# Rounded products for the query and key/value projections, and more weight halves split by an adding DMA

## The chip, the cores and the metric

The kernel runs on one core of one Trainium2 chip, as one launch. The metric is device time in microseconds (us), the median of several runs. All matrix products are done by TensorE (PE in the profile), elementwise work by VectorE (DVE) and ScalarE (ACT), transfers from the chip's memory (HBM) by 16 DMA engines; SyncE (SP) and GpSimd (POOL) only issue transfers here, apart from a few memsets.

## What is computed

Two networks stand one behind the other: a block with a convolution branch, an attention branch and a convolved feed-forward network, then a two-layer network with attention and a linear recurrence. Only the first part of the first block is touched by the change:

```python
h = rms_norm(x, norm1_g[l])
proj = h @ w_in[l]
a_in, q_c, kv_c, k_rope_in, gates = split_cols(proj, IN_SPLITS)
y_conv = conformer_conv(a_in, ...)          # gate, 31-tap depthwise conv, layer norm, silu, w_conv_out
# mla: 8 heads, q and kv from normalised low-rank parts
q  = (rms_norm(q_c, q_norm_g) @ w_uq)       # 384 -> 8 heads of 96
kv = (rms_norm(kv_c, kv_norm_g) @ w_ukv)    # 256 -> 8 heads of 64 + 64
...
g = jax.nn.sigmoid(gates)
merged = g[..., :D_MODEL] * y_conv + g[..., D_MODEL:] * y_mla
```

There are 256 tokens of width 1024; everything is float32.

## The kernel before

**Weights as one stream.** Every weight matrix is cut into blocks of 128 x 128, and the blocks lie in HBM (`wall`) in the order in which TensorE uses them (`PLAN`, L190). Sixteen blocks are a unit (1 MB) and eight a half (512 KB). `Stream` (L219) loads units into three buffers named `raw` (L229, issued by SP), and makes of each half two tiles `wh` and `wl` (L285, six buffers of each). `wh` is the weight rounded to the format fp32r, `wl` the rest that the rounding left out.

**Three rounded products or one native.** `product` (L442) takes a block and an operand that has been split in the same way into `xh` and `xl`, and issues three matmuls: wh by xh, wl by xh, wh by xl. For the matrices in `NATIVE` (L35: `w_uq` and `w_ukv`) the half is not split: the tile `raw` itself is multiplied by the unsplit operand in one float32 matmul, which TensorE runs as two records in the trace. The raw buffer of such a half becomes free only when TensorE has taken its last block (L349), that of a split half when the split is done (L314).

**Two ways to split.** Normally ACT rounds the half into `wh` (L254) and DVE subtracts (L255). For a half in `BY_DMA` (L307 to L311) ACT rounds it (L308) and writes the negative of the rounded half into `wl` (L309), and then POOL issues a DMA that reads the same half from HBM again and adds it on the way in, so that DVE has nothing to do.

**Looking ahead.** `ahead(look)` (L331) is called before and after the eight blocks of a column. It issues the splits of as many halves as `look` allows beyond the half in use: 4 as a rule (`LOOK`), 6 for `w_uq`, `w_ukv` and the gates (`N_SPLIT`). A split can start on the chip only when the half six places earlier has been used up, since there are six buffers.

**Order.** TensorE and SP run in the order of the program. For ACT, DVE and POOL a planner orders the instructions when the kernel is built; instructions marked by `paced` (L612) keep their order among each other. The 31 convolution taps of each of 4 channels (L621, on DVE) are taken from a list a few at a time, after each column of matmuls (`n_bg`, from `NB`), and they are paced.

**The stretch in question**, by halves in their order of use:

| halves | what TensorE does | lines |
|---|---|---|
| 0 to 7 | value and gate columns of the convolution branch (`w_a`) | L631 |
| 8 to 13 | five columns for `qc` and one for the rotary key | L668, L681 |
| 14 to 16 | `w_uq`, 8 heads of 3 blocks, native | L711 |
| 17, 18 | `w_ukv`, keys (256 wide) and values (512 wide), native | L721, L729 |
| 19 to 34 | 16 gate columns `w_g`, two after each head's scores | L817, L824 |
| 35 to 38 | `w_mla`, in a group of 4 columns and four of 1 | L859 |
| 39 on | `w_co`, the convolution branch's output | L861 |

After the `w_a` columns the query and key/value factors (`csq`, `kvr`, L691) are worked out by short ACT and DVE steps. The query factor is multiplied in afterwards (L714), while the key/value part of `qc` is multiplied beforehand (L699), so that `w_ukv` can only start behind it. Each head's and each gate's result has a PSUM buffer of its own (eight buffers of 512 columns, of which 256 are used), one DVE instruction that takes it out (L714, L821), and for the gates a tanh on ACT (L822).

**The layer norm of the convolution** is `ln_mean` (L791), ahead of `w_mla`, and `ln_rest` (L800), which TensorE meets between two groups of `w_mla` (`norm_conv`, L839: ahead of the first block of the group that begins with column 4). `ln_rest` sums the squares `usq` by TensorE, and then a chain on ACT and DVE ends in the split of `cacc` into `uh` and `ul`, which `w_co` needs.

Of the kernel before, what the change touches and what calls it, by code (L numbers as in the profile page):

```python
# [13 lines left out]
ALU = mybir.AluOpType  # L14
# [4 lines left out]
P = 128  # L19
D = 1024  # L20
S = 256
# [6 lines left out]
HB = 8  # L28
N_RAW = 3
N_SPLIT = 6  # L30
# [1 line left out]
GELU_AT = 4  # L32
Y_AT = {4: (0,), 5: (1, 2), 6: (3, 4, 5), 7: (6, 7)}
REC_GATES = {5: (0, 1, 2), 6: (3, 4), 7: (5, 6)}
NATIVE = {"w_uq", "w_ukv"}  # L35

DMA_GATES = (0, 3, 5, 7, 9, 11, 13, 14, 15)
NB = (3, 3, 2, 1, 5, 6)
WARM = 12
SCAN_N = 2  # L40
# [7 lines left out]
HEADS = 8  # L48
# [163 lines left out]


ITEMS = items()
GATE0 = next(i for i, e in enumerate(PLAN) if e[0] == "w_g") // HB
BY_DMA = {GATE0 + m for m in DMA_GATES}


class Stream:  # L219
# [135 lines left out]
def build(tc, wall, x_t, meta_t, pos, vec, cst, gw, g_fin, out):  # L355
    nc = tc.nc
    ctx = ExitStack()
    with ctx:
# [55 lines left out]
        def split(src, hi, lo):  # L414
            nc.scalar.copy(out=hi, in_=src)
            nc.vector.tensor_tensor(out=lo, in0=src, in1=hi.bitcast(F32), op=ALU.subtract)  # L416
# [15 lines left out]
        def tt(out_, a, b, op=ALU.mult):  # L432
            return nc.vector.tensor_tensor(out=out_, in0=a, in1=b, op=op)  # L433
# [18 lines left out]
        def linear(name, col, xs, nk, out_, n_bg=0, look=LOOK):  # L452
            w.ahead(look)
            for k in range(nk):
                product(out_, (name, k, col), xs(k), k == 0, k == nk - 1)
            w.ahead(look)
            for _ in range(min(n_bg, len(bg))):
                bg.popleft()()
# [153 lines left out]
        def paced(i):  # L612
            tc.stamp_issue_order_token(i.ins, "conv")
# [53 lines left out]

        for m in range(5):  # L668
            p_ = mm_tile()
            linear("w_a", m * P, xa, 8, p_[:, :S], n_bg=NB[1])  # L670
            g = v("q_norm_g", m) if m < 3 else v("kv_norm_g", m - 3)
            act(out=qc[:, m, :], in_=p_[:, :S], func=AF.Identity, scale=g)
            s_ = pt([P, S], "sqq", bufs=3)
            act(out=s_, in_=p_[:, :S], func=AF.Square)
            if m < 3 and "w_uq" not in NATIVE:
                split(qc[:, m, :], qh[:, m, :], ql[:, m, :])
            if m > 1:
                add_sq(m - 2)
            sqs.append(s_)
        kr_p = mm_tile()  # L680
        linear("w_a", 5 * P, xa, 8, kr_p[:, :S], n_bg=NB[1])  # L681
        csr = pt([P, S], "csr")
        tt(csr, cs, rstd[:, :S])
        krp = pt([P, S], "krp")
# [10 lines left out]
            rsqrt_row(q[:, :S], dst, n)  # L695
        tt(csq, csq, csr)
        tt(kvr, kvr, rstd[:, :S])
        for m in range(3, 5):
            tt(qc[:, m, :], qc[:, m, :], kvr)  # L699
            if "w_ukv" not in NATIVE:  # L700
                split(qc[:, m, :], qh[:, m, :], ql[:, m, :])

        def xq(k):
            return qc[:, k, :] if "w_uq" in NATIVE else (qh[:, k, :], ql[:, k, :])
# [3 lines left out]

        tables("exp_and_others")

        for h in range(HEADS):  # L711
            p_ = mm_tile()
            linear("w_uq", h * P, xq, 3, p_[:, :S], n_bg=NB[2], look=N_SPLIT)
            paced(stt(qp[:, h, :], p_[:, :S], MLA_SCALE, csq, ALU.mult, ALU.mult))  # L714

        kr2 = psum("tr", 2)
        mm(kr2[:, :S], c("comb"), krp, True, True)
# [96 lines left out]
                    split(cacc[:, k, :], uh[:, k, :], ul[:, k, :])  # L814

        es, pts = {}, {}
        def gate_out(i):  # L817
            p_ = mm_tile()
            linear("w_g", (14 + i) * P, xa, 8, p_[:, :S], n_bg=NB[4 + (i > 3)], look=N_SPLIT)
            dst = t1[:, i, :] if i < 8 else t2[:, i - 8, :]  # L820
            paced(tt(dst, p_[:, :S], rstd[:, :S]))  # L821
            act(out=dst, in_=dst, func=AF.Tanh, scale=0.5)  # L822

        for h in range(8):  # L824
            es[h] = scores(h)
            if h % 2 and h > 1:
                pv_mla((h - 3) // 2)
            if h:
                pts[h - 1] = transposes(es.pop(h - 1))
            gate_out(2 * h)  # L830
            gate_out(2 * h + 1)
        while bg:
            bg.popleft()()
        pts[7] = transposes(es.pop(7))
# [2 lines left out]
        uh, ul = pt([P, 5, S], "qh", F32R), pt([P, 5, S], "ql", F32R)  # L837

        def norm_conv(m, k):  # L839
            if m == 4 and k == 0:  # L840
                ln_rest()

        mh, ml = ph.tile([P, 8, S], F32R, tag="kp", name="mh"), ph.tile([P, 8, S], F32R, tag="qp", name="ml")
# [665 lines left out]
```

## Time and profile before

| | |
|---|---|
| device time, median of 3 runs | 964.12 us (963.01 to 965.53) |
| the profiled execution's own time | 966.51 us |
| its span | 964.7 us, 17922 instructions |
| mean granted TensorE clock | 0.997 |
| DMA | 168.58 MB, mean 175 GB/s |

The span is cut into 40 slices on the page; each digit is the busy share of the slice in tenths. The stretch in question lies in slices 2 to 7 (24 us each), and DVE is the busiest engine beside TensorE there:

```profile
PE   9998999999999999999999999999999999999997
PEld 8988999999999999999999999999999999998886
DVE  6997978799999665866786555455577986667986
ACT  7758868677666655555556666444469776776552
```

Busy time of TensorE in this profile includes the overlap of pipelined matmuls, so the waits and the chain that ended last say more than its share. Times in the views count from the start of the span.

### The profile page before, as it was taken

How to read it: one execution, taken by the hardware profiler on the slowest of the kernel's cores; microseconds unless marked ns; L12 is line 12 of the kernel's file. 1: busy time of each engine (PE TensorE's matmuls, PEld its weight loads, DVE VectorE, ACT ScalarE, POOL GpSimd, SP SyncE). 2: the span in 40 equal slices, each digit the busy share in tenths (PEclk: the TensorE clock that was granted, in tenths of full speed). 3: DMA queues.
4: the chain of work that ended last, by engine and by line, in shares of the span. 5: the costliest groups of instructions: out<-in, count | busy, mean ns of one | idle time of the engine just before them, and what ended most of it. 6: DMA issues, size and time to landing. Idle time of an engine off the chain costs nothing.

```text
span 964.7 us, 17922 instructions
## 1 busy us (share of the span) xinstructions
PE 949.8 (98%) x7315; PEld 916.7 (95%) x7315; DVE 728.1 (75%) x1264; ACT 614.8 (64%) x1042; POOL 14.5 (2%) x47
## 2 busy tenths in 40 slices
PE   9998999999999999999999999999999999999997
PEld 8988999999999999999999999999999999998886
DVE  6997978799999665866786555455577986667986
ACT  7758868677666655555556666444469776776552
POOL 0001100000000000000000000000000000000000
PEclk9999999999999999999999999999999999999999
DMA  8559844546545555332325554445443465563561
GB/s 307 201 147 295 211 151 157 186 167 214 179 176 188 191 191 175 132 127 96 128 97 209 175 175 176 176 175 175 175 175 132 141 237 191 175 207 127 197 212 44
DMA packets 27874, 168.58 MB, mean 175 GB/s; under 512 B 4048, under 2 KB 6032, under 8 KB 8720
## 3 DMA queue, kind: packets, MB, share of 16 engines
q1 hardware_dynamic: 25312, 160.29, 47.1%
q0 software_dynamic: 1584, 6.29, 3.1%
q10 hardware_dynamic: 896, 0.86, 0.4%
q8 instruction: 57, 0.93, 0.4%
q14 instruction: 25, 0.20, 0.1%
HBM read 165.92 MB, written 1.05 MB: 173 GB/s over the span
## 4 chain that ended last, share of the span: by engine, by line
PE 91%; DVE 4%; DMA 2%; ACT 2%; issue 0%; SPq 0%; DVEq 0%; ACTq 0%; POOLq 0%
PE ps_mm L439 85%; PE ps_z L439 3%; PE ps_o L439 1%; DMA wl<-wall 1%; DVE wl L255 1%; DMA raw<-wall 1%; PE ps_tr L439 1%; DVE iu L1231 0%; ACT L400 0%; DMA vec_t<-vec 0%; PE ps_tr L770 0%; DVE gt L433 0%; ACT wh L254 0%; DVE iu L433 0%; DVE th L436 0%
## 5 line engine op out<-in xcount | busy, mean ns | idle before, releaser
L255 DVE TENSOR_TENSOR wl<-raw,wh 128x1024 fp32r<-128x1024 f32 (+1 forms) x287 | 343.4, 1201 | 162.3 <-ACT wh L254 161.3
L254 ACT CAST wh<-raw 128x1024 fp32r<-128x1024 f32 (+1 forms) x287 | 293.6, 1030 | 192.8 <-PE ps_mm L439 185.1
L439 PE MATMUL ps_mm<-Ah,wh 128*128 128x256 f32 (+1 forms) x1424 | 408.9, 287 | 1.0 <-ACT Ah L404 1.0
L439 PE MATMUL ps_mm<-Ah,wl 128*128 128x256 f32 (+1 forms) x1424 | 405.1, 285 | 3.1 <-DMA wl<-wall 3.1
L439 PE MATMUL ps_mm<-Al,wh 128*128 128x256 f32 (+1 forms) x1424 | 403.8, 284 | 0.0
L439 PEld LDWEIGHTS ps_mm<-Ah,wl 128*128 128x128 f32 x1424 | 268.4, 188 | 4.0 <-DMA wl<-wall 3.3
L439 PEld LDWEIGHTS ps_mm<-Ah,wh 128*128 128x128 f32 x1424 | 267.9, 188 | 2.0 <-ACT Ah L404 1.4
L439 PEld LDWEIGHTS ps_mm<-Al,wh 128*128 128x128 f32 x1424 | 269.3, 189 | 0.4 <-DVE Al L424 0.4
L439 PE MATMUL ps_mm<-hl,wh 128*128 128x272 f32 (+1 forms) x432 | 123.5, 286 | 0.0
L439 PE MATMUL ps_mm<-hh,wh 128*128 128x272 f32 (+1 forms) x432 | 123.5, 286 | 0.0
L439 PE MATMUL ps_mm<-hh,wl 128*128 128x272 f32 (+1 forms) x432 | 123.3, 285 | 0.0
L439 PEld LDWEIGHTS ps_mm<-hh,wl 128*128 128x128 f32 x432 | 81.3, 188 | 0.0
L439 PEld LDWEIGHTS ps_mm<-hh,wh 128*128 128x128 f32 x432 | 81.3, 188 | 0.0
L439 PEld LDWEIGHTS ps_mm<-hl,wh 128*128 128x128 f32 x432 | 81.3, 188 | 0.0
L621 DVE SCALAR_TENSOR_TENSOR cacc<-upad,whalf,cacc 128x256 f32<-128x256 f32 x120 | 57.4, 479 | 2.0
L404 ACT ACTIVATE ta<-ps_mm 128x272 f32<-128x272 f32 (+1 forms) x64 | 25.0, 391 | 49.9 <-PE ps_mm L439 49.8
L439 PE MATMUL ps_mm<-wh,hh 128*128 128x512 f32 (+1 forms) x127 | 48.8, 384 | 0.0
L439 PE MATMUL ps_mm<-wl,hh 128*128 128x512 f32 (+1 forms) x127 | 48.8, 384 | 0.0
L439 PE MATMUL ps_mm<-wh,hl 128*128 128x512 f32 (+1 forms) x127 | 48.7, 384 | 0.0
L439 PE MATMUL ps_mm<-bl,wh 128*128 128x256 f32 (+1 forms) x160 | 45.7, 286 | 0.6 <-DVE bl L416 0.6
L439 PE MATMUL ps_mm<-bh,wh 128*128 128x256 f32 (+1 forms) x160 | 46.1, 288 | 0.0
L439 PE MATMUL ps_mm<-bh,wl 128*128 128x256 f32 (+1 forms) x160 | 45.5, 284 | 0.0
(257 smaller groups left out, 1234.7 us busy)
## 6 DMA issues: line engine op xcount, KB each, us to landing
raw<-wall SPq DMA_DIRECT2D x148, 1024.0 KB, 4.9
wl<-wall POOLq DMA_DIRECT2D x9, 512.0 KB, 8.1
raw<-wall SPq DMA_DIRECT2D x3, 512.0 KB, 8.4
raw<-wall SPq DMA_DIRECT2D x4, 256.0 KB, 5.8
xres<-x_t SPq DMA_DIRECT2D x4, 256.0 KB, 6.0
gw_t<-gw POOLq DMA_DIRECT2D x1, 1024.0 KB, 7.6
wide<-g_fin POOLq DMA_DIRECT2D x1, 512.0 KB, 6.8
out_t<-gx SPq DMA_DIRECT2D x2, 256.0 KB, 2.2
```

Source lines behind the costliest of these rows:

```text
L254: self.nc.scalar.copy(out=hi[:, r], in_=src[:, r])
L255: self.nc.vector.tensor_tensor(out=lo[:, r], in0=src[:, r], in1=hi[:, r].bitcast(F32), op=ALU.subtract)
L404: i = nc.scalar.activation(out=out, in_=in_, func=func, **kw)
L439: nc.tensor.matmul(out=out_, lhsT=lhsT, rhs=rhs, start=start, stop=stop, skip_group_check=True)
L621: paced(nc.vector.scalar_tensor_tensor(out=cacc[:, ch, :], in0=upad[:, ch, j:j + S], scalar=wj, in1=cacc[:, ch, :], op0=ALU.mult, op1=ALU. ...
```

## The change

`NATIVE` becomes empty: `w_uq` and `w_ukv` take the three rounded products, their operand `qc` is split into `qh` and `ql` (one instruction pair for the three query parts, one for the two key/value parts), and their five halves 14 to 18 are split too. The set of halves split by the adding DMA is written out: 9, 11, 13 and 14 to 18 are new, half 19 leaves it, and 22, 24, 26, 28, 30, 32, 33 and 34 stay; that is 16 halves in place of 9. The `w_a` columns for halves 8 to 13 look ahead by 5 in place of 4. Heads and gates share a PSUM buffer in pairs, and are taken out by one instruction of 512 columns per pair. `ln_rest` moves from the second group of `w_mla` into the first, ahead of its third step.

```diff
-NATIVE = {"w_uq", "w_ukv"}
-DMA_GATES = (0, 3, 5, 7, 9, 11, 13, 14, 15)
+NATIVE = set()
+BY_DMA = {9, 11, 13, 14, 15, 16, 17, 18} | {19 + m for m in (3, 5, 7, 9, 11, 13, 14, 15)}
...
-GATE0 = next(i for i, e in enumerate(PLAN) if e[0] == "w_g") // HB
-BY_DMA = {GATE0 + m for m in DMA_GATES}
...
         for m in range(5):
             p_ = mm_tile()
-            linear("w_a", m * P, xa, 8, p_[:, :S], n_bg=NB[1])
+            linear("w_a", m * P, xa, 8, p_[:, :S], n_bg=NB[1], look=5)
...
-            if m < 3 and "w_uq" not in NATIVE:
-                split(qc[:, m, :], qh[:, m, :], ql[:, m, :])
+            if m == 2 and "w_uq" not in NATIVE:
+                split(qc[:, 0:3, :], qh[:, 0:3, :], ql[:, 0:3, :])
...
-        for m in range(3, 5):
-            tt(qc[:, m, :], qc[:, m, :], kvr)
-            if "w_ukv" not in NATIVE:
-                split(qc[:, m, :], qh[:, m, :], ql[:, m, :])
+        tt(qc[:, 3:5, :], qc[:, 3:5, :], kvr[:, None, :].to_broadcast([P, 2, S]))
+        if "w_ukv" not in NATIVE:
+            split(qc[:, 3:5, :], qh[:, 3:5, :], ql[:, 3:5, :])
...
-        for h in range(HEADS):
+        for h in range(0, HEADS, 2):
             p_ = mm_tile()
-            linear("w_uq", h * P, xq, 3, p_[:, :S], n_bg=NB[2], look=N_SPLIT)
-            paced(stt(qp[:, h, :], p_[:, :S], MLA_SCALE, csq, ALU.mult, ALU.mult))
+            for i in range(2):
+                linear("w_uq", (h + i) * P, xq, 3, p_[:, i * S:(i + 1) * S], n_bg=NB[2], look=N_SPLIT)
+            paced(stt(qp[:, h:h + 2, :], p_.rearrange("p (i k) -> p i k", i=2), MLA_SCALE,
+                      csq[:, None, :].to_broadcast([P, 2, S]), ALU.mult, ALU.mult))
...
-        def gate_out(i):
+        def gates_out(i):
             p_ = mm_tile()
-            linear("w_g", (14 + i) * P, xa, 8, p_[:, :S], n_bg=NB[4 + (i > 3)], look=N_SPLIT)
-            dst = t1[:, i, :] if i < 8 else t2[:, i - 8, :]
-            paced(tt(dst, p_[:, :S], rstd[:, :S]))
+            for j in range(2):
+                linear("w_g", (14 + i + j) * P, xa, 8, p_[:, j * S:(j + 1) * S], n_bg=NB[4 + (i > 3)],
+                       look=N_SPLIT)
+            dst = t1[:, i:i + 2, :] if i < 8 else t2[:, i - 8:i - 6, :]
+            paced(tt(dst, p_.rearrange("p (j k) -> p j k", j=2), rstd[:, None, :S].to_broadcast([P, 2, S])))
             act(out=dst, in_=dst, func=AF.Tanh, scale=0.5)
...
         def norm_conv(m, k):
-            if m == 4 and k == 0:
+            if m == 0 and k == 2:
                 ln_rest()
```

More of the change, by code (lines that the diff above doesn't have):

```diff
@@ L680, in build @@
         kr_p = mm_tile()
-        linear("w_a", 5 * P, xa, 8, kr_p[:, :S], n_bg=NB[1])
+        linear("w_a", 5 * P, xa, 8, kr_p[:, :S], n_bg=NB[1], look=5)
         csr = pt([P, S], "csr")
@@ L829, in build @@
                 pts[h - 1] = transposes(es.pop(h - 1))
-            gate_out(2 * h)
-            gate_out(2 * h + 1)
+            gates_out(2 * h)
         while bg:
```

## The prediction

> **What bounds the kernel now.** I read the page's shares of the chain that ended last first, then that chain in order of time, then TensorE's waits, and last the busy times by stage.
>
> ```profile
> PE 91%; DVE 4%; DMA 2%; ACT 2%; issue 0%; SPq 0%; DVEq 0%; ACTq 0%; POOLq 0%
> ```
>
> TensorE is 91% of the chain: a microsecond taken from its queue early in the span is kept to the end, unless a later wait swallows it. The chain in order of time through the changed stretch (start, us, what, how many):
>
> ```profile
> 47.87 2.85 PE ps_mm L439 x24
> 50.72 0.86 PE ps_tr L439 x4
> 51.58 10.36 PE ps_mm L439 x48
> 61.94 0.43 PE ps_tr L439 x2
> 62.37 6.89 PE ps_mm L439 x24
> 69.26 0.86 PE ps_z L439 x4
> 70.12 2.86 PE ps_mm L439 x24
> 73.06 10.37 DMA wl<-wall
> 83.47 4.22 PE ps_mm L439 x23
> 87.69 1.18 PE ps_z L439 x4
> ```
>
> The first row is a half in rounded products: 24 matmuls in 2.85 us, 0.119 us each. The rows at 51.58 and 62.37 are the native stage, 17.25 us: `w_uq` as 48 records, then `w_ukv` as 24 (16 of 256 columns, 8 of 512). At 73.06 the chain leaves TensorE: an adding DMA, the one for half 22, took 10.37 us, and TensorE went on at 83.47. What this cost is seen in TensorE's waits and the windows (length, busy times of PE, PEld, DVE, ACT, POOL, clock, DMA share, GB/s):
>
> ```profile
> PEld ps_mm L439 <- DMA wl<-wall: 3.3, 1, 3.3
> ...
> PEld ps_mm L439 <- ACT qh L415: 0.9, 1, 0.9
> ```
>
> ```profile
> 10.00:20.00 10.00, 9.63 (x76) 9.02 (x76) 8.29 (x17) 8.35 (x16) 0.78 (x1) 1.00 1.02 404
> ...
> 80.00:90.00 10.00, 6.92 (x43) 6.50 (x42) 6.60 (x14) 6.95 (x15) 0.86 (x1) 0.83 1.04 321
> ```
>
> One wait of 3.3 us, and behind it a mean clock of 0.83: the 23 matmuls from 83.47 took 4.22 us where 23 x 0.119 = 2.73 are normal, and the four score matmuls 1.18 in place of 0.86 (row at 69.26). So the wait cost 3.3 + 1.5 + 0.3 = 5.1 us. The second wait, 0.9 us, is for `qh` at the start of `w_co`.
>
> Why half 22 was late is in SP's waits:
>
> ```profile
> SPq L237 <- PE ps_mm L439: 20.9, 2, 13.9
> ```
>
> Twice SP stood 20.9 us in all before a load, for TensorE: these are the raw buffers that the native halves 14 to 17 hold until used. Behind them unit 11 (halves 22, 23) came late, and ACT's two steps and the DMA after it.
>
> **The change part by part.** *Native to rounded products.* `w_uq` has 24 blocks, the keys of `w_ukv` 8: (24 + 8) x 3 x 0.119 = 11.4 us against 10.36 + 16 x 10.36/48 = 13.8. The values have 4 matmuls of 512 columns, which become 12. A rounded product of that width is bounded by the chain's last long row:
>
> ```profile
> 873.72 84.45 PE ps_mm L439 x381
> ```
>
> 0.222 us each, 2.7 us in all, against 6.89 - 3.45 = 3.4. Together **-3.2 us**, all on the chain.
>
> *The gate wait.* Halves 14 to 18 now give their raw buffers back when ACT has read them, five halves ahead of their use, so units 10 and 11 load sooner, by about half of SP's 20.9 us each (an estimate); half 22's DMA was 3.3 us late. **-5.1 us.** The term is firm in its 3.3; the 1.8 of clock may be absent in other runs. The Trainium skill, "TensorE: Matmul & The Clock Gate", Part 1, says that the clock halves after an idle window of about 3.4 us and that the window runs freely; the trace's loss after a wait of 3.3 us agrees nearly. By that rule a wait of this size is sometimes unpunished and the term would be -3.3.
>
> *`ln_rest` earlier.* Its chain now has some three halves of time more before `w_co`, so the wait for `qh` goes: **-0.9**. Could TensorE wait at the new place instead?
>
> ```profile
> 138.35 1.06 ACT L404 ACTIVATE upad<-cacc 128x1024 f32<-128x1024 f32 x1 [1.03 <-DVE cacc L433]
> ```
>
> The squares end at 139.41. The chain has TensorE begin `w_mla` at 136.67, and eight blocks later it is 139.52. It just holds; 0 to 1 us, I take 0. The ACT and DVE work is the same, and what it overtakes there are casts for halves with time in hand.
>
> *Weight splits.* The groups of the first 330 us (busy us, mean ns):
>
> ```profile
> L255 DVE TENSOR_TENSOR wl<-raw,wh 128x1024 fp32r<-128x1024 f32 x88 | 107.1, 1221 | 21.3 <-ACT wh L254 20.5
> ...
> L309 ACT ACTIVATE wl<-raw 128x1024 fp32r<-128x1024 f32 x9 | 9.5, 1053 | 1.4 <-PE ps_mm L439 1.4
> L308 ACT CAST wh<-raw 128x1024 fp32r<-128x1024 f32 x9 | 9.4, 1042 | 5.1 <-PE ps_mm L439 3.0 <-DMA raw<-wall 2.1
> ...
> L311 POOL DMA_DIRECT2D wl<-wall x9 | 7.9, 878 | 85.9 <-ACT csq L404 31.4 <-ACT wl L309 21.4 <-PE ps_mm L439 20.2
> ...
> L433 DVE TENSOR_TENSOR t<-ps_mm,rstd 128x256 f32<-128x256 f32 x16 | 6.6, 418 | 3.5 <-PE ps_mm L439 3.5
> ...
> L255 DVE TENSOR_TENSOR wl<-raw,wh 128x512 fp32r<-128x512 f32 x4 | 2.6, 685 | 0.5 <-ACT wh L254 0.5
> ```
>
> DVE loses three subtractions and gains one, -2.4 us. Heads and gates, 24 x 0.418 = 10.0, become 12 x 0.685 (a 512-column subtraction; the instruction is another) = 8.2. The operand splits add about 0.7 + 0.95 (768 columns lie between 0.685 and 1.221). Net about -2.5. ACT gains 5 x 2.1 for halves 14 to 18 and 3 x 1.05 for 9, 11, 13, less 1.05: +12.6, and 1.5 for operand casts; pairing the tanhs gives a little back. None of this is itself on the chain; it is hidden behind TensorE while ACT keeps ahead. The wider look only lets halves 13 to 18 stand one place earlier in ACT's order, and a shared PSUM buffer is held longer, but there are fewer in use. DVE is nearly full already:
>
> ```profile
> 20.00:130.00 110.00, 106.85 (x769) 98.80 (x769) 102.95 (x220) 79.73 (x147) 8.25 (x10) 0.98 0.73 217
> ```
>
> 102.95 of 110 us; afterwards about 100.5 in some 104. The taps are paced and end before `ln_mean`, so I cost DVE at 0; up to 2 us if softmax steps queue behind taps and the transposes wait. POOL issues 16 in place of 9, 0.88 each, in order: nothing on its queue besides.
>
> *Half 9, the new wait.* What counts is ACT's second step, then POOL, then the landing:
>
> ```profile
> 26.32 1.99 ACT L254 CAST wh<-raw 128x1024 fp32r<-128x1024 f32 x2
> ```
>
> ```profile
> 35.12 0.29 PE L439 MATMUL ps_mm<-Ah,wl 128*128 128x256 f32 x1
> ```
>
> ```profile
> DMA to landing us min/median/max: 5.9/8.5/12.2
> ```
>
> ```profile
> wl<-wall POOLq DMA_DIRECT2D x9, 512.0 KB, 8.1
> ```
>
> The casts at 26.32 are halves 8 and 9. Half 9's `wl` step would end near 28.3 + 1.0 = 29.3, and TensorE wants that tile at 35.1. With 5.9 us to land it comes at 35.2; with 8.1, the median of all nine, at 37.4; with 12.2 (the longest in 50 to 100 us), at 41.5. The DMA engines are 0.73 busy over 20 to 130, so I do not count on the shortest and take 8.1: **+2.3** (0 to 6.4, and up to 1.8 of clock from about 3.3 on). TensorE's queue stands behind it: all later halves shift, which gives their DMAs time.
>
> *Halves 11 to 18 and the key/value operand.* DMA load in 28 to 130 us:
>
> ```profile
> q1 hardware_dynamic: 2304, 16.78, 46.0%
> q0 software_dynamic: 1296, 4.72, 24.7%
> ```
>
> An adding DMA costs 102 x 0.247 / 9 = 2.8 us of all 16 engines, a raw half 102 x 0.46 x 0.524 / 16.78 = 1.5. From half 13 to 18 each half needs 4.3 us of DMA in 2.85 us of TensorE: 8.5 us short over six halves, if nothing ran ahead. But each half's tile is free 14.25 us (five halves) before its use, and the engines had room there:
>
> ```profile
> 40.00:50.00 10.00, 10.00 (x82) 9.84 (x81) 9.75 (x22) 6.17 (x11) 0.00 (x0) 1.00 0.31 107
> 50.00:60.00 10.00, 10.00 (x51) 8.89 (x50) 9.89 (x27) 5.62 (x11) 1.02 (x1) 1.00 0.37 61
> ```
>
> DMA shares of 0.31 and 0.37, ACT busy 11.8 of 20. With the ten steps of halves 14 to 18 and the operand casts, less half 19's two, ACT comes to 11.8 + 9.9 = 21.7 of 20: full, and half 18's second step ends near 57 (an estimate); landed at 65.1, while TensorE, shifted by 2.3, wants it at 65.7.
>
> The Trainium skill, "DMA: Bandwidth & Descriptors", Specifications, puts a core's HBM limit at about 358 GB/s. The row 10 to 20 shows 404, so the trace does not agree. By that page's figure the six halves (1.05 MB in 2.85 us each, 368 GB/s) would be only 0.5 us short.
>
> The key/value operand is on a chain of its own:
>
> ```profile
> 58.70 0.75 DVE L433 TENSOR_TENSOR qc<-qc,kvr 128x256 f32<-128x256 f32 x2
> ```
>
> Ready at 59.45 now, with TensorE asking at 62.37; after, the cast and the subtraction follow (0.6 + 0.7), 60.8, shifted to 63, and TensorE asks at 51.58 + 2.3 + 8.55 + 0.43 = 62.9. For both together I take **+1.0** (0 to 5).
>
> **Sum:** -3.2 - 5.1 - 0.9 + 2.3 + 1.0 = -5.9 us. The profiled execution's own time is 966.51 (span 964.7), 2.4 above the median; the sum made against it gives 960.6, and carried to the median 964.12 it gives **958.2**.
>
> **Rivals.**
> - *All DMAs hidden:* the planner finds ACT time for half 9 sooner, and the lead of five halves holds: -9.2, 954.9. For it: a landing of 5.9 us would do. Against: the 8.1 at a busy 0.73.
> - *The clock loss was the profile's own:* the sum without its 1.8: -4.1, 960.0. For it: the profiled time lies above all runs shown.
> - *Half 9 late:* landing as in the chain's 10.37 row, at 39.7: 4.6 and 1.8 of clock in place of 2.3: -1.8, 962.3.
> - *The gate wait stays*, the change failing to bring unit 11 sooner: -5.9 + 5.1 = -0.8, 963.3. Against: nothing else in SP's waits holds that load.
> - *Slower: adding DMAs bunch.* In 13 to 18 the 8.5 us of missing DMA time fall on TensorE, beside half 9's 2.3 and one clock loss of 1.8: 12.6 - 9.2 = +3.4, 967.5. It decides once waits for `wl` exceed 9.2 us in all. For it: a DMA share of 1.04 with landings of 12.2 us where only every second half is added. Against: the lead, and room before.
>
> **How the numbers follow.** Forecast 0.42, all hidden 0.16, no clock loss 0.12, half 9 late 0.12, gate wait stays 0.07, bunching 0.11. The bound of what can be told from no change is 0.3%, 2.9 us: faster means below 961.2. The first three lie there: 0.70. Half 9 late and the gate wait are within it: 0.19. Bunching is slower: 0.11. The range 954.0 to 964.5 leaves out the bunching and the far end of the hidden case.
>
> **What would show it.** In the profile after: no wait for `wl` near 80 us and a clock of 1.00 in 80 to 90; the native rows gone, `w_uq` in about 8.6 us; SP no longer waiting for TensorE; a wait for a DMA `wl` at about 35 us of 2 us; at most short ones near 60 to 65; no wait for `qh` of `cacc`. I am wrong if the waits for DMA `wl` sum to over 6 us, if a wait for `usq` appears in `w_mla`, or if transposes wait for `es` because DVE fell behind.

## The result, and the profile after

| | before | after |
|---|---|---|
| device time, median | 964.83 us (963.01 to 965.92, 4 runs) | 971.19 us (970.83 to 971.76, 4 runs) |
| profiled execution | 966.51 us, span 964.7 | 971.33 us, span 969.5 |
| ratio of the times | | 1.0068, 95% interval 1.0051 to 1.0086 |

The change makes the kernel 0.7% slower; forecast were 958.2 us and a range of 954.0 to 964.5. The profiled execution of the kernel before lies 1.7 us above its median and that of the change only 0.1, so the two spans differ by 4.8 us where the medians differ by 6.4. Line numbers in this part of the code are two lower than before (L437 is the matmul, L306 and L307 are ACT's two steps for a half that is added by DMA, L309 is the DMA's issue, L413 and L414 split an operand). First the shares of the chain that ended last, on the page of the changed kernel:

```profile
PE 89%; DVE 4%; ACT 3%; DMA 2%; issue 2%; POOL 0%; SPq 0%; DVEq 0%; ACTq 0%; POOLq 0%
```

TensorE lost two points of the chain. Its waits in the first 200 us (total, times, longest) say to what:

```profile
PEld ps_mm L437 <- DMA wl<-wall: 5.4, 1, 5.4
PEld ps_mm L437 <- ACT qh L413: 3.9, 1, 3.9
...
PEld ps_mm L437 <- DVE ql L414: 0.4, 1, 0.4
```

The old waits (3.3 us for half 22's DMA, 0.9 us for `qh` of `cacc`) are gone. In their place stand 5.4 us for another adding DMA, and 3.9 us for a `qh`, which is now the key/value operand. The busy times by stage show where (length, PE, PEld, DVE, ACT, POOL, clock, DMA share, GB/s):

```profile
30.00:40.00 10.00, 5.77 (x49) 5.57 (x47) 9.86 (x24) 9.89 (x15) 2.75 (x3) 0.96 0.98 304
40.00:50.00 10.00, 9.02 (x55) 8.96 (x56) 7.08 (x16) 6.83 (x12) 1.67 (x2) 0.70 1.05 287
50.00:60.00 10.00, 10.00 (x80) 9.79 (x80) 5.63 (x13) 9.12 (x14) 2.62 (x4) 1.00 1.04 257
60.00:70.00 10.00, 8.84 (x73) 8.43 (x71) 8.67 (x17) 7.57 (x13) 0.00 (x0) 1.00 1.03 296
70.00:80.00 10.00, 7.41 (x36) 6.70 (x37) 9.19 (x18) 5.86 (x10) 0.86 (x1) 0.83 0.78 199
80.00:90.00 10.00, 10.00 (x79) 9.70 (x78) 8.75 (x18) 8.03 (x14) 1.73 (x2) 1.00 0.79 207
```

TensorE is busy 5.77 of 10 us from 30 to 40 and runs at a clock of 0.70 behind that; a second dent, with 0.83, lies at 70 to 80. From 80 to 90, where the dent was before, all is well. The DMA engines are full (0.98 to 1.05) over 40 us in which they had been at 0.31 and 0.37 in part. The chain in order of time (start, us, what):

```profile
30.08 10.86 DMA wl<-wall
40.98 8.08 PE ps_mm L437 x47
...
59.77 2.88 PE ps_mm L437 x24
62.68 1.05 ACT wh L252
...
71.70 0.63 ACT qh L413
72.35 0.70 DVE ql L414
73.10 7.19 PE ps_mm L437 x34
80.29 0.86 PE ps_z L437 x4
81.16 5.70 PE ps_mm L437 x48
...
142.60 3.07 PE ps_mm L437 x24
...
147.55 12.47 PE ps_mm L437 x104
```

Half 9's DMA is issued at 30.08 and lands at 40.94. The 47 matmuls behind it take 8.08 us; 48 of them take 5.70 in the row at 81.16, so the clock costs 2.5 us. At 62.68 the chain leaves TensorE for ACT, and comes back at 73.10, when the key/value operand is ready. The last rows run through `w_mla` into `w_co` with no hole: `ln_rest` moved without a wait.

What stood ahead of the operand is in ACT's own order of work (start, us, line, operation; in brackets the idle time before it, and what ended it):

```profile
28.70 1.05 ACT L307 ACTIVATE wl<-raw 128x1024 fp32r<-128x1024 f32 x1
...
62.68 1.05 ACT L252 CAST wh<-raw 128x1024 fp32r<-128x1024 f32 x1 [2.37 <-PE ps_mm L437]
63.63 0.50 ACT L402 ACTIVATE rt<-xn,eps_t 128x256 f32<-128x256 f32 x1
...
70.24 1.05 ACT L307 ACTIVATE wl<-raw 128x1024 fp32r<-128x1024 f32 x1
...
71.70 0.62 ACT L413 CAST qh<-qc 128x512 fp32r<-128x512 f32 x1
```

At 62.68 stands a cast for half 20, which can't start before TensorE has used up half 14: ACT waits 2.37 us with it, and the key/value factor's steps (`rt` at 63.63 and on) wait behind. Further casts, for halves 21 and 22, lie between the factor's steps, and so the 0.6 us cast that TensorE needs runs at 71.70.

**The account.** Gained: the products (3.0 us: in run e6_order below, where no wait for the operand stands between them, `w_uq` takes 8.63 in place of 10.36 and `w_ukv` 5.67 in place of 6.89), the gate wait 5.1, `ln_rest` 0.9, together 9.0. Paid: half 9 5.4 + 2.5 = 7.9, the operand 3.9 + 0.4 (`ql`) and 7.19 - 5.70 = 1.5 of clock (5.70 is the same row in run g1_no_add_order, at a clock of 1.00), 5.8. Together 13.7 - 9.0 = +4.7; the two spans differ by 4.8. Nothing large is missing between the two profiled executions.

### The profile page after: what moved, and what is told of

It reads as the page before. It is cut to its first block, busy times and chain, and to the rows that moved or that the text cites. A ratio compares the mean times of both kernels' runs of the same rounds, so it can differ in the third digit from the quotient of the medians.

```text
span 969.5 us, 18011 instructions
## 1 busy us (share of the span) xinstructions
PE 949.0 (98%) x7351; PEld 918.6 (95%) x7351; DVE 728.0 (75%) x1251; ACT 626.4 (65%) x1048; POOL 20.5 (2%) x54
## 3 DMA queue, kind: packets, MB, share of 16 engines
HBM read 169.59 MB, written 1.05 MB: 176 GB/s over the span
## 4 chain that ended last, share of the span: by engine, by line
PE 89%; DVE 4%; ACT 3%; DMA 2%; issue 2%; POOL 0%; SPq 0%; DVEq 0%; ACTq 0%; POOLq 0%
PE ps_mm L437 83%; PE ps_z L437 3%; DMA wl<-wall 1%; PE ps_o L437 1%; DVE wl L253 1%; DMA raw<-wall 1%; PE ps_tr L437 1%; DVE iu L1231 0%; ACT wh L252 0%; PE ps_tr L769 0%; ACT L398 0%; DMA vec_t<-vec 0%; DVE gt L431 0%; DVE iu L431 0%; DVE th L434 0%
## 5 line engine op out<-in xcount | busy, mean ns | idle before, releaser
L437 PE MATMUL ps_mm<-Ah,wl 128*128 128x256 f32 (+1 forms) x1424 | 405.7, 285 | 5.4 <-DMA wl<-wall 5.2
L437 PE MATMUL ps_mm<-Ah,wh 128*128 128x256 f32 (+1 forms) x1424 | 409.3, 287 | 1.4 <-ACT Ah L402 1.4
L437 PE MATMUL ps_mm<-Al,wh 128*128 128x256 f32 (+1 forms) x1424 | 404.2, 284 | 0.0
L437 PEld LDWEIGHTS ps_mm<-Ah,wl 128*128 128x128 f32 x1424 | 268.9, 189 | 6.3 <-DMA wl<-wall 5.4
L437 PEld LDWEIGHTS ps_mm<-Ah,wh 128*128 128x128 f32 x1424 | 268.3, 188 | 2.6 <-ACT Ah L402 1.9
L437 PEld LDWEIGHTS ps_mm<-Al,wh 128*128 128x128 f32 x1424 | 269.9, 190 | 0.7 <-DVE Al L422 0.7
L437 PE MATMUL ps_mm<-hl,wh 128*128 128x272 f32 (+1 forms) x432 | 123.5, 286 | 0.0
L437 PE MATMUL ps_mm<-hh,wh 128*128 128x272 f32 (+1 forms) x432 | 123.4, 286 | 0.0
L437 PE MATMUL ps_mm<-hh,wl 128*128 128x272 f32 (+1 forms) x432 | 123.3, 285 | 0.0
L437 PEld LDWEIGHTS ps_mm<-hh,wl 128*128 128x128 f32 x432 | 81.3, 188 | 0.0
L437 PEld LDWEIGHTS ps_mm<-hh,wh 128*128 128x128 f32 x432 | 81.3, 188 | 0.0
L437 PEld LDWEIGHTS ps_mm<-hl,wh 128*128 128x128 f32 x432 | 81.3, 188 | 0.0
L437 PE MATMUL ps_mm<-wh,hh 128*128 128x512 f32 (+1 forms) x127 | 48.8, 384 | 0.0
L437 PE MATMUL ps_mm<-wl,hh 128*128 128x512 f32 (+1 forms) x127 | 48.8, 384 | 0.0
L437 PE MATMUL ps_mm<-wh,hl 128*128 128x512 f32 (+1 forms) x127 | 48.7, 384 | 0.0
L437 PE MATMUL ps_mm<-bl,wh 128*128 128x256 f32 (+1 forms) x160 | 45.7, 286 | 0.6 <-DVE bl L414 0.6
L437 PE MATMUL ps_mm<-bh,wh 128*128 128x256 f32 (+1 forms) x160 | 46.2, 289 | 0.0
L437 PE MATMUL ps_mm<-bh,wl 128*128 128x256 f32 (+1 forms) x160 | 45.5, 284 | 0.0
```

What stands on the lines that cost most here:

```text
L437: nc.tensor.matmul(out=out_, lhsT=lhsT, rhs=rhs, start=start, stop=stop, skip_group_check=True)
```

## The experiments

Each run is compared with runs of the kernel before on the same chip. In the last column DMA is an adding DMA's `wl`, `qh` and `ql` are the operand's two parts, and `es` is a step of the softmax; each number is the total of the first 200 us of the profiled execution.

| run | median us | ratio to before (95%) | TensorE's largest waits, us |
|---|---|---|---|
| e1_no9 | 971.02 | 1.0062 (1.0047 to 1.0077) | DMA 5.9, qh 3.9 |
| e2_before_9 | 969.22 | 1.0052 (1.0035 to 1.0069) | DMA 5.7 |
| e6_order | 969.58 | 1.0049 (1.0034 to 1.0064) | DMA 6.0, es 3.6 |
| e7_no9_order | 969.83 | 1.0055 (1.0040 to 1.0070) | DMA 6.5, es 3.6 |
| f1_no_add | 964.25 | 0.9986 (0.9975 to 0.9998) | qh 3.9 |
| f2_pool_neg | 971.95 | 1.0067 (1.0048 to 1.0085) | DMA 5.4, es 2.3, qh 1.9 |
| f3_dve_split | 968.06 | 1.0029 (1.0017 to 1.0041) | qh 4.5, es 4.0, ql 2.0 |
| f5_before_gates | 964.90 | 0.9994 (0.9983 to 1.0005) | es 3.9 |
| g1_no_add_order | 965.07 | 1.0002 (0.9992 to 1.0012) | es 3.6 |
| g2_no_add9 | 968.09 | 1.0028 (1.0011 to 1.0045) | DMA 4.5, qh 3.9 |
| g3_native_gates | 961.40 | 0.9963 (0.9950 to 0.9975) | es 1.5 |
| g4_native_parts | 963.34 | 0.9983 (0.9974 to 0.9992) | DMA 2.1 |
| h1_balance | 967.49 | 1.0025 (1.0014 to 1.0036) | es 5.4, DMA 2.8 |
| h2_kv_rounded | 968.20 | 1.0034 (1.0022 to 1.0045) | qh 4.9, es 4.2 |
| h3_q_rounded | 968.57 | 1.0043 (1.0030 to 1.0055) | es 6.3, DMA 4.5 |
| i1_kv_vec | 970.40 | 1.0061 (1.0047 to 1.0075) | ql 4.6, es 3.6 |
| i2_after_vec | 971.58 | 1.0072 (1.0059 to 1.0085) | DMA 5.2, qh 3.8 |
| i3_kv_first | 968.42 | 1.0037 (1.0024 to 1.0050) | DMA 5.6 |

### Half 9 alone

```diff
-BY_DMA = {9, 11, 13, 14, 15, 16, 17, 18} | {19 + m for m in (3, 5, 7, 9, 11, 13, 14, 15)}
+BY_DMA = {11, 13, 14, 15, 16, 17, 18} | {19 + m for m in (3, 5, 7, 9, 11, 13, 14, 15)}
```

> The changed kernel with one edit: half 9 goes back to ACT and DVE and is not split by the adding DMA. Theory A, two independent waits: the 5.4 us wait at 35 us and the 2.7 us of half clock behind it go, the wait for the key/value operand stays near 4.3 us; 971.2 - 8.1 = about 963. Theory B, the key/value operand is bound by ACT's queue in absolute time: TensorE only arrives there sooner, that wait grows by 4 us or more; 967 to 971.

971.02 us: no gain. The wait at 35 us is gone, and 5.9 us of waits for adding DMAs stand near 50, for halves 13 and 14. POOL's order of work, and below it the landing times of the adding DMAs in that stretch:

```profile
43.16 1.78 POOL L309 DMA_DIRECT2D wl<-wall  x2 [8.27 <-DVE cacc L619]
46.25 0.86 POOL L309 DMA_DIRECT2D wl<-wall  x1 [1.30 <-DVE cacc L619]
```

```profile
DMA to landing us min/median/max: 8.2/15.4/17.8
```

In this kernel the second steps of these halves came late in ACT's order, and three DMAs were issued within 4 us; they took up to 17.8 us to land. The first lands at 53.35; in the change, half 9's wait and its clock had shifted TensorE by 8 us, and it began half 13 only at 56.06. Neither theory as stated: the wait moved.

The other way round, half 9 by DMA in the kernel before:

```diff
-BY_DMA = {GATE0 + m for m in DMA_GATES}
+BY_DMA = {9} | {GATE0 + m for m in DMA_GATES}
```

> The kernel before with half 9 alone added to the halves split by the adding DMA. Theory A, the DMA is issued too late for its landing whatever else runs (raw loads suffice to make it long): it lands after 9 to 11 us, TensorE waits 3.5 to 5.5 us at 35 us and loses 1.7 to 2.7 us of clock; 970 to 973. Theory B, it was long only because the adding DMAs of halves 11, 13 and 14 shared the engines: it lands in 6 to 7.5 us, TensorE waits under 2 us; 965 to 967.

969.22 us, 4.7 over before. DMA waits of 5.7 us in two: half 9's 4.2, with a clock of 0.88 in 40 to 50, and 1.5 of the old gate wait. The window from 30 to 40, of the kernel before and of this run:

```profile
30.00:40.00 10.00, 10.00 (x86) 10.00 (x85) 10.00 (x23) 8.00 (x14) 0.00 (x0) 1.00 0.75 279
```

```profile
30.00:40.00 10.00, 5.98 (x48) 5.77 (x47) 9.95 (x22) 6.37 (x11) 0.65 (x1) 0.95 1.01 310
```

Half 9's DMA lands after 9.7 us, and it alone brings the DMA share from 0.75 to 1.01. One half is late by itself, with none of the later halves added to the set: theory A, though the time is just below its range.

### The order on ACT

The casts of halves 19 to 22 are tied behind the table load that follows the key/value factor:

```diff
         w = Stream(nc, wall, raw_pool, split_pool)
+        w.stamp = lambda h, i: tc.stamp_issue_order_token(i.ins, "tables") if 19 <= h <= 22 else None
...
-            self.nc.scalar.copy(out=hi[:, r], in_=src[:, r])
+            i = self.nc.scalar.copy(out=hi[:, r], in_=src[:, r])
+            self.stamp(h, i)
```

> The changed kernel with ACT's casts of halves 19 to 22 held in program order behind the table load that follows the key/value factor, so that none of them stands ahead of that factor's steps. Theory A, the wait for the key/value operand is ACT's queue order (a cast ahead of the chain waits for TensorE to free a buffer): it falls from 4.3 to under 1.5 us and the half clock behind it goes; 965 to 967. Theory B, the chain is long of itself, or DVE's queue sets it: the wait stays over 3.5 us; 970 to 971.

969.58 us. The wait for the operand's `qh` is gone (it was 3.9), so the order on ACT was its cause. Of the 5.8 us that it had cost, 1.6 come back, less than theory A had; a wait for `es`, the softmax, is new:

```profile
PEld ps_tr L771 <- ACT es L404: 3.6, 2, 3.3
```

The same with half 9 by VectorE (the two edits above together):

> Both edits: half 9 by ACT and DVE, and the casts of halves 19 to 22 behind the key/value factor. Theory A: both waits go, leaving the gains; 971.2 - 8.1 - 5 = about 958, faster than both kernels. Theory B, ACT's load sets the operand in absolute time: a wait of 3 us or more for it remains; 962 to 967.

969.83 us: DMA waits of 6.5 us for halves 13 and on, and the 3.6 for `es`. Two mended places, two new ones of the same size.

### The adding DMAs

The addition of halves up to 18 is left out, with all of ACT's steps kept, so that the low parts of these halves stay incomplete:

```diff
-                self.nc.gpsimd.dma_start(out=lo, in_=self.w[a][:, o * P:(o + HB) * P], accum_op=ALU.add)
+                if h > 18:
+                    self.nc.gpsimd.dma_start(out=lo, in_=self.w[a][:, o * P:(o + HB) * P], accum_op=ALU.add)
```

> The changed kernel without the adding DMAs of halves 9, 11 and 13 to 18: ACT still writes both tiles, so its load and order stay, and what is left out is the addition, so that the low parts of these eight halves are wrong. Theory A, the DMA's landing is what TensorE pays for at 35 us: the waits for wl go with their half clock (8.1 us), the operand wait of about 4.3 us stays or grows little; 962 to 965. Theory B, ACT's queue sets the whole stretch and the DMA waits only stand in for it: another wait of 4 us or more takes the place; 967 to 971.

964.25 us, 6.9 less than the change: no wait for a DMA is left, and the 3.9 us for `qh` stays. The adding DMAs of these eight halves cost 7 us. Half 9's addition alone left out (`if h != 9`):

> The changed kernel without the adding DMA of half 9 alone (its addition is left out; ACT's work and order as in the change). Theory A, the engines' rate: with TensorE 5 us sooner, the DMAs of halves 11 to 16 come late in its place, 4 us or more of waits for wl again; 968 to 971. Theory B, half 9's late launch alone: the others land in time, no wait for wl of over 1.5 us; 963 to 966.

968.09 us: 3.1 less, where half 9's wait and its clock came to 7.9. The next one, half 11, now makes TensorE wait 4.5 us:

```profile
32.53 12.11 DMA wl<-wall
44.68 4.51 PE ps_mm L438 x23
```

So it is not half 9 alone that lands late, but each one issued in this stretch. Without the additions and with ACT's order tied as in e6_order:

> The changed kernel without the adding DMAs of halves 9, 11 and 13 to 18 (their addition is left out) and with ACT's casts of halves 19 to 22 in program order behind the key/value factor. Theory A, landing and ACT's order are the two costs and together eat the gains: with both away the forecast's gains show, 958 to 960. Theory B, as in the run with the order alone, a softmax step takes the operand's place, because ACT has too much in front of TensorE's next want whatever the order: a wait of 3 us or more for es, 962 to 965.

965.07 us, no better than f1_no_add, although the operand is in time (a wait of 1.7 us for `qh` and `ql`). ACT's order of work shows the next in line:

```profile
82.17 1.06 ACT L308 ACTIVATE wl<-raw 128x1024 fp32r<-128x1024 f32 x1 [1.69 <-PE ps_mm L440]
83.14 0.61 ACT L405 ACTIVATE t<-t 128x512 f32<-128x512 f32 x1
...
85.49 0.91 ACT L405 ACTIVATE es<-es,rs 128x256 f32<-128x256 f32 x2
```

ACT stands 1.69 us before a `wl` step whose buffer TensorE still uses; the softmax steps stand behind it, and TensorE waits for them 3.3 us. It is the picture of 62.68 in the change again, at another place. The key/value projection's matmuls, with the clock at full speed, are read from this run's chain:

```profile
62.99 5.70 PE ps_mm L440 x34
```

### Other engines for the same work

ACT's second step, for halves up to 18, by GpSimd:

```diff
-                self.nc.scalar.mul(out=lo, in_=src, mul=-1.0)
+                if h > 18:
+                    self.nc.scalar.mul(out=lo, in_=src, mul=-1.0)
+                else:
+                    self.nc.gpsimd.tensor_scalar(out=lo, in0=src, scalar1=-1.0, scalar2=None, op0=ALU.mult)
```

> The changed kernel with the second step of the adding halves up to 18 (writing the negative into wl) on GpSimd in place of ACT: ACT loses 8 instructions of 1.05 us, DMA stays. Theory A, DMA landing: the wait at 35 us stays at 4 to 7 us and others of its kind may come; 966 or more. Theory B, ACT's load: the operand wait falls under 1.5 us and DMAs are issued sooner; 964 or less.

971.95 us: ACT's load falls, the time does not. GpSimd needs 3.3 us a half for what ACT does in 1.05, and VectorE slows down beside it (below). Then halves 9, 11 and 13 to 18 by ACT and DVE, with no addition (`BY_DMA = {19 + m for m in (3, 5, 7, 9, 11, 13, 14, 15)}`):

> The changed kernel with halves 9, 11 and 13 to 18 split by ACT and DVE, so that only the eight gate halves use the adding DMA. DVE gains 8 x 1.22 = 9.8 us, ACT loses 8.4, DMA 8 x 2.8. Theory A, the adding DMAs are the cause of the loss: the wait at 35 us goes and the forecast's gains show; 957 to 962. Theory B, DVE, nearly full before, becomes the bound: waits for wl by DVE or for softmax steps of 6 us or more; 965 to 971.

968.06 us. No DMA wait is left, but DVE has no idle time for 30 us, and the operand and the softmax fall behind. One window of this run (40 to 60 have 10.00 and 9.98 for DVE):

```profile
60.00:70.00 10.00, 4.21 (x18) 3.77 (x18) 9.96 (x20) 4.62 (x7) 1.02 (x1) 0.70 0.82 196
```

### Without the rounded projections

In the kernel before, halves 22 and 24 by VectorE and `ln_rest` moved:

```diff
-DMA_GATES = (0, 3, 5, 7, 9, 11, 13, 14, 15)
+DMA_GATES = (0, 7, 9, 11, 13, 14, 15)
...
-            if m == 4 and k == 0:
+            if m == 0 and k == 2:
```

> The kernel before with two edits of its own: gate halves 22 and 24 split by ACT and DVE in place of the adding DMA, and the second part of the layer norm in the first group of w_mla as in the change. Theory A, the wait at 80 us was the late raw unit plus the DMA's landing: without the landing the half is there in time, 5.1 us go, and 0.9 for the layer norm; 964.5 - 6 = 958.5, faster than both. Theory B, the raw unit alone is late or half 26's DMA is next in line: a wait of 2 us or more stays; 961 to 964.

964.90 us, no difference. Both old waits are gone, and `es` makes TensorE wait 3.9 us in six, with a clock of 0.83 from 120 to 130: DVE took on two subtractions and its softmax steps came late. In the change, heads and gates are taken out in pairs, which gives DVE time back. With the projections native, and the pairs, the moved `ln_rest` and the wider look of the change kept, first with the halves added as before (g4_native_parts, the diff), then with half 22 by VectorE too, that is without the 3 in the set (g3_native_gates):

```diff
-NATIVE = set()
-BY_DMA = {9, 11, 13, 14, 15, 16, 17, 18} | {19 + m for m in (3, 5, 7, 9, 11, 13, 14, 15)}
+NATIVE = {"w_uq", "w_ukv"}
+BY_DMA = {19 + m for m in (0, 3, 5, 7, 9, 11, 13, 14, 15)}
```

> The change without its products and its new set of adding DMAs: pairs, layer norm and wider look alone, all halves split as before. Theory A: only the wait before w_co goes, 0.9 us; 963 to 965. Theory B: pairs give DVE some 2 us and that shows in TensorE's time too; 960 to 962.

> The change without its products and new adding DMAs: both projections native as before, pairs and layer norm as in the change, and of the nine gate halves split by DMA only half 22 goes to ACT and DVE. Theory A: the 5.1 us at 80 us go, 0.9 for the layer norm, and the pairs give DVE back what half 22 costs it, so that softmax steps wait for under 1.5 us; 957 to 961, faster than both kernels. Theory B, DVE is the bound behind the gates, as in the run on the kernel before with two gate halves moved: waits for es of 3 us or more; 963 to 966.

963.34 (theory A) and **961.40 us** (theory A by its waits, the time 0.4 above its range), the fastest of all kernels here: 0.9963 of before (0.9950 to 0.9975). The first still waits 2.1 us for half 22's DMA. In the second no wait of TensorE in the first 200 us is longer than 1.3 us, and the clock is 1.00 in every window from 20 to 150 us. Its waits, and its busy times where the kernel before had its dent:

```profile
PEld ps_tr L769 <- ACT es L402: 1.5, 2, 1.3
```

```profile
80.00:90.00 10.00, 10.00 (x82) 9.79 (x81) 9.71 (x21) 9.98 (x22) 1.72 (x2) 1.00 0.95 256
```

Against g4_native_parts, which has the rest of the change, the rounded projections with the new set of halves by DMA cost 971.19 - 963.34 = 7.9 us; the two medians are from different chips, on which the kernel before agreed within 0.2 us.

### Placing or amount?

All three rounded, the low parts dealt out between DMA and VectorE, order tied as in e6_order (`BY_DMA = {11, 14, 16, 18} | {19 + m for m in (0, 5, 7, 9, 11, 13, 14, 15)}`):

> All three products rounded, as in the change, with the low parts dealt out: halves 11, 14, 16 and 18 by an adding DMA, 9, 13, 15 and 17 by VectorE, half 22 by VectorE too, and the casts of halves 19 to 22 behind the key/value factor's steps. Theory A (the named waits are the whole cost: half 9's landing, the operand behind ACT's casts, and each new one is a matter of placing): with half 9 and 22 out of the DMA and the order mended no wait over 2 us is left, and the three terms of the prediction, -9.2, show nearly whole: 956 to 960. Theory B (the stretch from 20 to 130 us has no room on any of the three for the splits of five more halves, however they are dealt out): waits of 3 us or more appear again, for a DMA, for es or for a split by VectorE: 963 to 968.

967.49 us: better than the change by 3.7, with a wait of 5.1 us for `es` (theory B). Then only one of the projections on top of g3_native_gates: `NATIVE = {"w_uq"}` with half 18 added, and `NATIVE = {"w_ukv"}` with 14 and 16 added:

> The fastest kernel so far (query and key/value projection native, pairs, earlier rest of the layer norm, half 22 by VectorE), with the key/value projection alone in rounded products: halves 17 and 18 are split, 18 by an adding DMA. TensorE loses 0.6 us on the keys and 0.75 on the values. Theory A (room enough for two halves, only placing matters): 959.5 to 960.5, below 961.4. Theory B (no room even for two halves, and the operand's cast and subtraction stand in front of the keys): the gain is given back by a wait for ql, qh or the DMA of 2 us or more, 962 to 966.

> The fastest kernel so far, with the query projection alone in rounded products: halves 14, 15 and 16 are split, 14 and 16 by an adding DMA, and the key/value projection stays native. TensorE loses 10.36 - 24 x 3 x 0.119 = 1.8 us. Theory A (room for three halves): 959 to 960.2. Theory B (no room): the gain is given back and more by a wait for wl or for es, 962 to 967.

968.20 and 968.57 us: over g3_native_gates, two halves cost 6.8 us and three 7.2, where all five, dealt out as in h1_balance, cost 6.1. Both lie above even theory B's ranges, with waits of the kind that it named, but the trace of the first doesn't show a lack of engine time. ACT's order of work in it:

```profile
63.46 1.99 ACT L252 CAST wh<-raw 128x1024 fp32r<-128x1024 f32 x2 [6.49 <-DMA raw<-wall]
65.36 0.61 ACT L413 CAST qh<-qc 128x512 fp32r<-128x512 f32 x1
```

ACT stood idle 6.49 us, before a cast for a load that was late, and the operand's cast stood behind it. So the next run takes that cast off ACT:

```diff
-            split(qc[:, 3:5, :], qh[:, 3:5, :], ql[:, 3:5, :])
+            split_v(qc[:, 3:5, :], qh[:, 3:5, :], ql[:, 3:5, :])
```

> The kernel of the run before with the key/value projection alone rounded, in which ScalarE stood 6.5 us before a cast of a later half whose raw load was late, with the key/value operand's cast queued behind it (TensorE waited 4.9 us for qh). Here the operand's cast is done by VectorE, just ahead of its subtraction, so it stands behind no weight split on ScalarE; all else is the same. Theory A (order: the operand stood behind a cast that had to wait, and the load that it waited for is needed much later): no wait for qh; TensorE's wait there under 1 us, the softmax steps' wait for es falls back towards the 1.5 us of the native kernel, 959.5 to 962. Theory B (amount: the stretch has no room for two more halves): the same loss under another name, a wait for a split, es or a DMA of 3 us or more: 965 to 969.

970.40 us, worse, and above both ranges. DVE's order of work:

```profile
59.26 0.42 DVE L417 CAST qh<-qc 128x512 fp32r<-128x512 f32 x1
64.40 1.23 DVE L253 TENSOR_TENSOR wl<-raw,wh 128x1024 fp32r<-128x1024 f32 x1 [4.72 <-ACT wh L252]
65.54 0.68 DVE L418 TENSOR_TENSOR ql<-qc,qh 128x512 fp32r<-128x512 f32 x1
```

The operand's `qh` is ready before 60, as it should be, but its `ql` stands behind a subtraction for a later half, which waits for ACT's cast, which waits for the load: the same blockage, one queue further. The same edit in the change itself:

> The change as it is, with the key/value operand's cast done by VectorE in place of ScalarE: one step moved, no weight split moved with it. Theory A (the 4.3 us wait and its 1.7 us of half clock come from the place in ScalarE's queue alone): the wait for qh is gone, half 9's 5.4 us stays, and the time falls by 4 to 6 us, 965 to 967.5. Theory B (the wait covers the others: whatever is late behind it comes up instead): a wait of 3 us or more appears in 60 to 95 us, 968.5 to 971.

971.58 us, nothing gained: here the factor's own steps stand behind the casts on ACT, and the operand is ready at 73.0 as in the change. Last, the order alone: the kernel of h2_kv_rounded, with the operand's cast first, then the table load, then the casts of halves 19 to 22:

```diff
+            i = nc.scalar.copy(out=qh[:, 3:5, :], in_=qc[:, 3:5, :])
+            tc.stamp_issue_order_token(i.ins, "tables")
+            tt(ql[:, 3:5, :], qc[:, 3:5, :], qh[:, 3:5, :].bitcast(F32), ALU.subtract)
```

> The kernel with the key/value projection alone rounded (968.2), with nothing moved to another engine and no work taken away: only the order on ScalarE is tied, so that the key/value operand's cast comes first, then the table load of exp, then the casts of halves 19 to 22. VectorE's subtraction for the operand then also stands ahead of those of halves 20 and 21. Theory A (order: what TensorE waited 4.9 and 4.6 us for in the two runs before was a short step queued behind a split of a later half that waited for its load): the operand is ready near 60 us, no wait for qh or ql, and the 5 us with their half clock come back: 959.5 to 962. Theory B (amount): a wait of 3 us or more for a split, es or a DMA instead, 965 to 969.

968.42 us. The operand is in time; the chain shows what is late instead:

```profile
64.27 11.32 DMA wl<-wall
75.63 8.19 PE ps_mm L439 x47
```

Half 19, whose casts now stand behind the operand's, is given to its DMA at 64.27, some 11 us later than in h2_kv_rounded, where ACT had done its two steps by 52.7, and lands at 75.59. From 50 to 60 ACT was busy only 4.49 of 10 us, but part of its idle time is a wait for DVE, which was busy 9.86 there:

```profile
60.02 0.62 ACT L700 CAST qh<-qc 128x512 fp32r<-128x512 f32 x1 [3.18 <-DVE qc L433]
```

So this run doesn't separate order from amount: DVE had next to no room. And the order was tied too tightly: the casts that held up the operand in h2_kv_rounded were those of halves 20 and 21, and half 19, whose steps on ACT were long done there, is made to wait here for no gain. An order with half 19 ahead and only 20 to 22 behind the operand wasn't tried.

## Why the prediction was wrong

**Right.** The products (forecast -3.2, measured -3.0). The gate wait (-5.1): none near 80 us, clock 1.00 in 80 to 90; SP's queue no longer waits for TensorE. `ln_rest` (-0.9): no hole before `w_co`. The gains of 9.2 came as worked out, within 0.2 us in the profiled executions. The rival in which the clock loss was the profile's own has something for it, though: the 33 recorded runs of the kernel before with a mean granted clock of 0.997 or less have a median of 965.9 us, the 51 with 0.998 or more 964.3. That fits the 1.8 us of clock being lost in part of the runs only, in which case the change had less to gain against the median than against the profiled execution. It isn't shown, since only one execution was profiled.

**The size of the miss.** The sum was -5.9 us, the spans differ by +4.8. Of these 10.7 us, 5.6 are half 9's term (7.9 in place of 2.3) and 4.8 the operand's (5.8 in place of 1.0).

**Half 9: the mechanism right, the size wrong.** Measured: ACT done at 29.75, issued at 30.08, 10.86 us to land, 5.4 us of wait and 2.5 of clock. Of the 3.5 us by which it came later than I had it, 0.8 are the issue and 2.8 the landing. The rival "half 9 late" had the landing within half a microsecond. I took the median landing of DMAs from other stages. The mean share of 0.73 that I went by was near that of the very window (0.75 from 30 to 40); what I left out is the transfer's own time on the engines. With the 2.8 us that I had worked out for an adding DMA the window comes to 1.03, and e2_before_9, with half 9's DMA alone, measured 1.01 and 9.7 us to land. The DMAs of halves 11 and 13, which the change issues at 33.94 and 38.39, are left with about 1.2 of the 10.86 us. g2_no_add9 and e1_no9 show that it belongs to the stretch, not to the half: with 9 out of the way, 11 or 13 and 14 are as late. That is the slower rival's mechanism (the adding DMAs bunch) in part; f1_no_add puts all of it at 7 us, where that rival had 12.6 with its clock.

**The operand: the step that failed.** I took +1.0 for halves 11 to 18 and the key/value operand together; in the change TensorE waits for none of these halves' DMAs, and the operand costs 5.8. I had its chain of short steps shifted with TensorE, and counted what ACT has to do (21.7 us of work in 20, "full"), but not in what order. ACT's rows show its steps one behind the other, and a planned cast for a half far ahead, whose buffer or load is not there yet, holds everything behind it. In the change that is one cast idle for 2.37 us and three halves' casts between the steps. e6_order shows it: with these casts behind the factor's steps, no wait for `qh` is left.

**DVE at 0, up to 2.** In the change itself that holds: from 20 to 150 us no wait for DVE or for `es` is longer than 0.4 us. But there was no reserve to speak of: with two more subtractions (f5_before_gates) or eight (f3_dve_split) TensorE waited for the softmax some 4 us in all.

**Why no single repair helped.** In seven runs one wait was taken away and another of 3 to 6 us came up (e1_no9, e6_order, e7_no9_order, g1_no_add_order, g2_no_add9, i1_kv_vec, i3_kv_first). A wait of TensorE gives everything behind it that much more time; taken away, the next late step shows. The split of a half needs a load, one or two steps on ACT, one on DVE or a DMA of about 11 us, each in a queue where other halves and the short steps of the critical factors and the softmax stand too.

**What stays open.** Whether there is an order of these queues in which the rounded projections pay at all. In h2_kv_rounded ACT stood idle before a load, with DVE busy 9.00 and 5.18 of 10 us from 50 to 70, so there it was not the mere amount of work; in i3_kv_first DVE was nearly full, and amount isn't ruled out. None of the orders tried was without a new wait, and how far a better planner would get wasn't tried. That waits are moved rather than removed is shown; that the 9 us could be had is not.

## What to carry to other kernels

Before a term is put at "hidden", read the queue of the engine that makes the operand, in order, and find the first instruction in it that itself waits for a buffer or a load: everything behind that one is late by as much, however idle the engine looks. A transfer's landing is to be taken from the window into which it is put, with its own time on the engines, and that of the transfers that the same change starts beside it, added to the share there: here the sum came to 1.03, and where the median of other stages was 8.1 us, the landing took 10.86. Where VectorE, ScalarE and the DMA engines each have little left, take the parts of a change that remove work or move it where there is time (here: taking out results in pairs and the earlier `ln_rest`, 0.2% in g4_native_parts) and leave those that add steps to full queues: the whole change costs 0.7%. With the time that the pairs free on DVE, half 22's low part, which the change leaves to its DMA, can go there too; that makes it 0.4% (g3_native_gates).

## What the hardware showed

**An adding DMA lands late under load.** The same 512 KB landed in 5.8 us when it was the only one between 24 and 75 us (g3_native_gates, at a DMA share of 0.40 from 50 to 60), in 10.7 at the median of the change (0.98 to 1.05 from 30 to 70), and in up to 17.8 in e1_no9.

**The clock falls behind a wait.** Behind 5.4 us of wait 47 matmuls took 8.08 us in place of 5.6; behind 4.3 us the key/value stage took 7.19 in place of 5.70. The Trainium skill, "TensorE: Matmul & The Clock Gate", Part 1, states that TensorE drops to half its clock after an idle window of about 3.4 us; these rows agree. The clock cost a third to a half of the wait on top of it, 1.5 for 4.3 us and 2.5 for 5.4. But a single wait of that length isn't needed: in f5_before_gates, where the longest wait from 110 to 130 is 2.0 us, the clock is 0.83 from 120 to 130, while behind the 2.1 us of g4_native_parts it stays at 1.00. These runs give no threshold.

**GpSimd slows VectorE.** In f2_pool_neg, where GpSimd does 25.9 us of tensor work between 20 and 75 us, the convolution's taps on DVE took 701 ns there at the mean; the kernel before has 477, the change 483. The rows, of the kernel before and of this run (busy us, mean ns):

```profile
L621 DVE SCALAR_TENSOR_TENSOR cacc<-upad,whalf,cacc 128x256 f32<-128x256 f32 x54 | 25.8, 477 | 0.7
```

```profile
L622 DVE SCALAR_TENSOR_TENSOR cacc<-upad,whalf,cacc 128x256 f32<-128x256 f32 x38 | 26.6, 701 | 0.6
```

In this run's order of work, one tap on DVE, and two halves on GpSimd that begin while it runs:

```profile
43.71 2.38 DVE L622 SCALAR_TENSOR_TENSOR cacc<-upad,whalf,cacc 128x256 f32<-128x256 f32 x1
```

```profile
44.08 6.20 POOL L310 TENSOR_SCALAR wl<-raw 128x1024 fp32r<-128x1024 f32 x2
```

A tap whose mean is 0.48 us in the kernel before took 2.38; others beside GpSimd's work keep 0.47, as at 35.41 beside an instruction from 33.12 to 36.60. The Trainium skill, "Trainium Architecture — The Big Picture", section "What this means for kernel authors", says that these two engines share a port pair under an exclusive lock; that single taps stand still while others keep their usual time fits a lock better than an even slow-down, though no row here shows the lock itself.
